# A fifth mixed pair in the second FFN's gate and up tiles, its weight sums made in the mixer

## The chip, the cores and the metric

The kernel runs on one core of one Trainium2 chip (trn2). The metric is the device time of one execution in microseconds (us). Five engines matter here: PE (TensorE, matrix products), DVE (VectorE), ACT (ScalarE), POOL (GpSimd) and SP (SyncE, which here only issues transfers). Each works through its own instructions in order and waits on semaphores that other engines and transfers set. Transfers run on 16 DMA engines that all queues share.

## The reference

One layer of a decoder over 272 positions (16 meta tokens, 256 sequence positions), model width 2048, in float32:

```python
h += 0.5 * swiglu(rms_norm(h, g1), w_gate1, w_up1, w_down1)      # first FFN, hidden width 5632
z  = rms_norm(h, gm) @ w_in                                      # q, k, v, index keys, conv and gate columns
h += (sigmoid(ga) * y_attn + sigmoid(gc) * y_conv) @ w_out       # sparse attention and short gated convolution
h += 0.5 * swiglu(rms_norm(h, g2), w_gate2, w_up2, w_down2)      # second FFN
swiglu(x, g, u, d) = (silu(x @ g) * (x @ u)) @ d
```

The result is `h` without the meta tokens.

## The kernel before

**Precision.** Every float32 weight is split into a high part (`whi`, made by ACT at L175) and the rest (`wlo`, made by DVE at L176), and every product is three matmuls (high times high, high times low, low times high), for instance L408 to L410 in `trio`. So each weight passes through SP (load into a `raw` buffer), ACT, DVE and PE. `Stream` (L109 on) keeps that order: weights come in *units* of at most 1024 columns. When PE's program takes a unit, `Stream.next` also emits the split of the unit three places further on (`AHEAD`). There are four pairs of `whi` and `wlo` buffers, three `raw` buffers of 1 MB, and a fourth (`raws`) in the second FFN. A load is issued once the split of the buffer's former weights is done.

**Extra work** is hung on the stream by unit number: `st.put` with a slot of `LAG` (the slot halved is the number of units to wait; even slots go before the split of that step in the engines' order, odd ones behind it), `st.later` likewise.

**The stages.** First FFN (to about 790 us), norm and keys (`pkv`), index queries (`pi`), queries (`pq`), convolution (`pxc`, `pcg`, `pb`), with the attention's small steps laid between, one a unit; then gates and branches, the output projection, and the second FFN from 1412 us.

**The second FFN** works on tiles of 512 columns, 6 and then 5 gate and up tiles (`GROUPS`), each group followed by its share of the down projection in two tiles. A gate and up tile takes the 2048 input features in eight *pairs* of 128-wide blocks. For a pair, gate and up for two blocks of 128 tokens are a 2 by 2 times 2 by 2 block product. A *plain* pair does it with eight products (24 matmuls of 512 columns, units named 0 and 1). A *mixed* pair does it in Winograd's way with seven (21 matmuls, units A to D, where A, C and D are 1024 columns and B is 512). For that it needs sums of the activations (`combos`: five sums on DVE, and splits of them on ACT and DVE, kept in `comb` and elsewhere), and sums of the weights: units A and B use three of the four weight blocks as they are (0.75 MB), C and D four sums (1 MB) that were made earlier and lie in DRAM scratch (`made`). When a tile's last mixed pair is through, `spread` and `gather` put the products together; then come silu, the product with up, two transposes and `move_blocks`, which writes the tile to DRAM (`hold<-mt`, POOL) and reads it back turned (four times `mt<-hold`, POOL).

**Which pairs are mixed** is the table `MIXED = 1, 3, 5, 6`; the very first tile mixes pair 5 alone. `order(n, mixed)` (L89) lists a tile's units in the pairs' order 0 to 7.

**The weight sums** are made by `job` (L554): a POOL transfer brings the 1 MB chunk into a buffer, four DVE operations of 128x512 (L568) make the sums, a POOL transfer writes them to scratch. `JOBS = 46` of the 57 jobs run in the first FFN, one every five units, with three buffers. The last 11 run behind the convolution.

Of the kernel before, what the change touches and what calls it, by code (L numbers as in the profile page):

```python
# [15 lines left out]
P = 128  # L16
# [9 lines left out]
H = 8  # L26
# [43 lines left out]
FIFTH = 4  # L70
FIVE = ()
LAST_MORE = 3, 4
JOBS_FROM = 24
JOBS_EVERY = 5
JOBS = 46
LATE_FROM = 4
LATE_EVERY = 6
# [5 lines left out]
    act_combos=(4, 12, 19, 32), factors=(7, 10, 12), out=(1, 1, 5, 17), act_split=(9, 14, 25, 33),  # L83
    below=(12, 17, 22, 30, 34), below_split=(15, 20, 30, 34, 35), fifth=(22, 25), late_below=(0, 5),
    late_split=(0, 6),
)


def order(n, mixed):  # L89

    out, i = [], 0
    while i < n:
# [4 lines left out]
        i += 1  # L97
    return out
# [137 lines left out]
def tile_decoder_layer(  # L236
# [53 lines left out]
    for g, n in enumerate(GROUPS):  # L290
        for f in range(n):
            now = sorted((*MIXED, *(FIFTH,) * ((g, f) in FIVE))) if gu else FIRST_MIXED
            sums = {i: scratch.tile([P, RAW], F32, name=f"made{gu + i}") for i in now}
            made += [(wgu2[gu + i], x) for i, x in sums.items()]
            for i, name in order(8, now):
                st.add_part(name, wgu2[gu + i], sums.get(i))
            gu += 8
        for d in (0, 2):
            now = down_mixed(g, d)
            sums = {i: scratch.tile([P, RAW], F32, name=f"sums{down + i}") for i in now}  # L300
            made += [(wd2[down + i], x) for i, x in sums.items()]
            for i, name in order(2 * n, now):
                st.add_part(name, wd2[down + i], sums.get(i))
            down += 2 * n
# [106 lines left out]

    def quads(c, m, x, mixed, n, after_mixed, tail=False):

        def of(k, j):
            return lambda part: x(k, j, part)

        plan, joined = [], []
        for i, name in order(n, mixed):
            k = 2 * i
            if name in "01":  # L420
                unit = [(c[j, q], of(k + int(name), j), 1 - q) for j in (1, 2) for q in (1, 0)]
                if tail and i == n - 1:
# [9 lines left out]
            plan.append((unit, i == max(mixed) and name == "D"))  # L432
# [120 lines left out]

    def job(pool, bufs, src, to, at, every, touch):  # L554
        box = {}

        def load():
            box["x"] = pool[0].tile([P, RAW], F32, name="made", bufs=bufs)
            if touch:
                nc.vector.tensor_copy(box["x"][:, :1], ones[:, :1])  # L560
            nc.gpsimd.dma_start(box["x"], src)

        def sums(n):
            b12, b11, b22, b21 = (box["x"][:, i * HALF : (i + 1) * HALF] for i in range(4))
            to, a, b, op = (
                (b22, b22, b12, "sub"), (b12, b12, b11, "sub"), (b11, b22, b11, "add"), (b21, b21, b11, "sub")
            )[n]
            getattr(nc.vector, f"tensor_{op}")(to, a, b)  # L568

        st.later(load, 1, at)  # L570
        for n in range(4):
            st.later(lambda n=n: sums(n), 1, at + every + n)
        st.later(lambda: nc.gpsimd.dma_start(to, box["x"]), 1, at + every + 4)

    def ffn_features():
# [3 lines left out]
        with tc.tile_pool(name="ffn1", bufs=2, reuse_waits="tile") as fp:  # L579
# [15 lines left out]

            for i, (src, to) in enumerate(made[:JOBS]):
                job([fp], 3, src, to, st.at + JOBS_FROM + i * JOBS_EVERY - 1, JOBS_EVERY, i < 3)

# [55 lines left out]
    def ffn_tokens():  # L654

        with ExitStack() as pools:
# [209 lines left out]
            for g, n in enumerate(GROUPS):  # L866
                for f in range(n):
# [15 lines left out]
                    quads(c, m, lambda k, j, part: known(("act", k // 4), act_tokens(k, j, part)), now, 8, lambda m=m: put(spread(m), LAG["spread"]))  # L883
                    put(gather(x, c), LAG["gather"])
# [29 lines left out]
                for d in (0, 2):  # L914
# [10 lines left out]

                    quads(c, m, middle_tokens, now, 2 * n, after, g and d)
                    put(gather_down(d, x, c, g == 1), LAG["drain"] if not g else 4 * (0,))
# [23 lines left out]
    with ExitStack() as mix:  # L951
# [250 lines left out]
        def scores(p, lag):  # L1202
            px = aux_tile("psc")
            for a in range(2):
                hh = 2 * p + a
                for j in (1, 2):
                    at = META * (2 - j)
                    nc.tensor.matmul(
                        px[:, a, SIDE[j]],
                        qT[:, hh, (j - 1) * P : j * P],  # L1210
                        kall[:, hh // (H // G), at : at + SEEN[j]],
# [69 lines left out]


        def q_steps():
            left = len(steps)
# [11 lines left out]
            new += [prep[3], tops[3], prep[4], tops[4], visit(prep[5], tops[5]), tops[6]]  # L1296
            new += [visit(*[lambda j=j: turn(qT, j) for j in (1, 2)]), tops[7], mask]
            for i in range(left):
# [46 lines left out]
        def conv_b(c, pb, y):  # L1345
            t = mw.tile([P, SEQ], F32, name="t", tag="cy")
            joined(t, pb)
            nc.vector.tensor_mul(y, t, y)
            to = cs[c // 4][:, c % 4]
            split_into(to[:, 0, :], to[:, 1, :], y)  # L1350

        for c in range(KC):
            box = {}
# [21 lines left out]
        st.later(jobs_pool, 3)  # L1375
        for i, (src, to) in enumerate(made[JOBS:]):
            job(jobs, 2, src, to, st.at + LATE_FROM + i * LATE_EVERY, LATE_EVERY, i < 2)

# [236 lines left out]
```

## Time and profile before

| | |
|---|---|
| time of 3 runs | 2108.28, 2108.98, 2109.17 us; median 2108.98 |
| profiled execution, first to last instruction | 2106.9 us |
| so outside the span, against the median of the runs | 2.1 us |
| granted PE clock | 1.00 |
| PE busy | 2098.8 us |
| DVE busy | 1582.4 us |
| ACT busy | 1058.9 us |
| bytes moved | 575.64 MB, 273 GB/s on average |

The profiled execution's own time is known only by its span. In the profile, a PE matmul of 512 columns is shown with a length of 0.39 us, but they overlap: one begins every 0.227 us. So the number of matmuls in a window is a better measure than their lengths. DVE and ACT operations of a row overlap a little too: two `wlo` in a row end 1.13 us apart where each is shown with 1.22 us. "L176" is a line of the kernel before; the changed kernel's lines lie a few further down.

### The profile page before, as it was taken

Reading aid. Unit: us, or ns where it says so; the run is one execution under the profiler, and the core shown is the slowest. Engines: PE = TensorE matmul, PEld = TensorE weight load, DVE = VectorE, ACT = ScalarE, POOL = GpSimd, SP = SyncE. Lnnn points to the kernel's source line nnn. Section 1 sums busy time; section 2 is a strip of 40 time slices with the busy share of each in tenths; the row PEclk is TensorE's granted clock in tenths of the full one; section 3 lists DMA queues with packets and bytes.
Section 4 is the critical chain, followed back from the end, with each engine's and each line's share of the span. In section 5 each row is a group of like instructions: output and inputs, shape, how many; then the busy total and the mean of one; then the engine's idle time right before and its main releaser. Section 6 shows DMA issues by size and latency. Waiting matters only on the chain.

```text
span 2106.9 us, 31863 instructions
## 1 busy us (share of the span) xinstructions
PE 2098.8 (100%) x12731; PEld 1889.9 (90%) x12731; DVE 1582.4 (75%) x2144; ACT 1058.9 (50%) x1342; POOL 106.0 (5%) x207
## 2 busy tenths in 40 slices
PE   9999999999999999999999999999999999999998
PEld 9999999999999999889988888888888888888887
DVE  7676766676776766578679678769788896878897
ACT  6444433344444445565444444456575565566654
POOL 0000000000000000000000000011000000000000
PEclk9999999999999999999999999999999999999999
DMA  7788888888888865445468886667988777799865
GB/s 265 260 320 327 324 315 322 311 337 310 322 313 325 328 224 177 164 159 181 152 216 329 323 301 223 219 233 255 314 314 300 281 268 247 282 306 319 306 250 207
DMA packets 85908, 575.64 MB, mean 273 GB/s; under 512 B 10112, under 2 KB 10880, under 8 KB 23808
## 3 DMA queue, kind: packets, MB, share of 16 engines
q1 hardware_dynamic: 64080, 438.34, 58.4%
q0 software_dynamic: 21104, 134.23, 17.1%
q8 instruction: 99, 1.62, 0.3%
q10 hardware_dynamic: 576, 1.05, 0.1%
q14 instruction: 49, 0.40, 0.1%
HBM read 504.90 MB, written 68.68 MB: 272 GB/s over the span
## 4 chain that ended last, share of the span: by engine, by line
PE 98%; DVE 1%; DMA 1%; issue 0%; ACT 0%; DVEq 0%; ACTq 0%
PE three L409 5%; PE three L408 5%; PE three L410 5%; PE pd L375 4%; PE pd L376 4%; PE pd L374 4%; PE pu L374 4%; PE pg L375 4%; PE pg L374 4%; PE pu L375 4%; PE pg L376 4%; PE pu L376 4%; PE pgt L402 3%; PE pgt L404 3%; PE pgt L403 3%; PE one L408 3%
## 5 line engine op out<-in xcount | busy, mean ns | idle before, releaser
L176 DVE TENSOR_TENSOR wlo<-raw,whi 128x1024 fp32r<-128x1024 f32 (+1 forms) x771 | 906.2, 1188 | 464.5 <-ACT whi L175 457.7
L175 ACT ACTIVATE whi<-raw 128x1024 fp32r<-128x1024 f32 (+1 forms) x771 | 786.4, 1030 | 883.4 <-PE pd L375 146.2
L375 PE MATMUL pd<-mid,whi 128*128 128x272 f32 x704 | 201.9, 287 | 0.0
L376 PE MATMUL pd<-mid,wlo 128*128 128x272 f32 x704 | 201.9, 287 | 0.0
L374 PE MATMUL pd<-mid,whi 128*128 128x272 f32 x704 | 201.9, 287 | 0.0
L374 PE MATMUL pu<-act,whi 128*128 128x272 f32 x672 | 192.8, 287 | 0.0
L376 PE MATMUL pu<-act,wlo 128*128 128x272 f32 x672 | 192.7, 287 | 0.0
L376 PE MATMUL pg<-act,wlo 128*128 128x272 f32 x672 | 192.7, 287 | 0.0
L375 PE MATMUL pg<-act,whi 128*128 128x272 f32 x672 | 192.7, 287 | 0.0
L375 PE MATMUL pu<-act,whi 128*128 128x272 f32 x672 | 192.7, 287 | 0.0
L374 PE MATMUL pg<-act,whi 128*128 128x272 f32 x672 | 192.7, 287 | 0.0
L568 DVE TENSOR_TENSOR made<-made 128x512 f32<-128x512 f32 x228 | 156.3, 685 | 0.0
L408 PE MATMUL three<-whi,act 128*128 128x512 f32 x352 | 137.2, 390 | 0.1
L409 PE MATMUL three<-wlo,act 128*128 128x512 f32 x352 | 137.0, 389 | 0.0
L410 PE MATMUL three<-whi,act 128*128 128x512 f32 x352 | 137.0, 389 | 0.0
L376 PEld LDWEIGHTS pd<-mid,wlo 128*128 128x128 f32 x704 | 132.7, 188 | 0.0
L374 PEld LDWEIGHTS pd<-mid,whi 128*128 128x128 f32 x704 | 132.7, 188 | 0.0
L375 PEld LDWEIGHTS pd<-mid,whi 128*128 128x128 f32 x704 | 132.7, 188 | 0.0
L176 DVE TENSOR_TENSOR wlo<-raws,whi 128x1024 fp32r<-128x1024 f32 x92 | 103.5, 1140 | 31.7 <-ACT whi L175 31.0
L374 PEld LDWEIGHTS pu<-act,whi 128*128 128x128 f32 x672 | 126.7, 188 | 0.0
L374 PEld LDWEIGHTS pg<-act,whi 128*128 128x128 f32 x672 | 126.7, 188 | 0.0
L376 PEld LDWEIGHTS pg<-act,wlo 128*128 128x128 f32 x672 | 126.6, 188 | 0.0
(381 smaller groups left out, 4482.7 us busy)
## 6 DMA issues: line engine op xcount, KB each, us to landing
raw<-in_wgu_dram SPq DMA_DIRECT2D x123, 1024.0 KB, 6.4
raw<-in_wd_dram SPq DMA_DIRECT2D x63, 1024.0 KB, 6.7
made<-in_wgu_dram POOLq DMA_DIRECT2D x41, 1024.0 KB, 10.6
made<-made POOLq DMA_DIRECT2D x41, 1024.0 KB, 6.5
raw<-made SPq DMA_DIRECT2D x31, 1024.0 KB, 6.1
raw<-in_wcv_dram SPq DMA_DIRECT2D x24, 1024.0 KB, 4.9
raw<-in_wgc_dram SPq DMA_DIRECT2D x24, 1024.0 KB, 5.1
raw<-in_wga_dram SPq DMA_DIRECT2D x24, 1024.0 KB, 5.4
```

The lines of the kernel that those rows point to most:

```text
L175: nc.scalar.activation(hi[:, :n], raw, AF.Copy)
L176: nc.vector.tensor_sub(lo[:, :n], raw, hi[:, :n].bitcast(F32))
L374: nc.tensor.matmul(ps, whi, xhi, start=first, stop=False)
L375: nc.tensor.matmul(ps, whi, xlo, start=False, stop=False)
L376: nc.tensor.matmul(ps, wlo, xhi, start=False, stop=last)
L402: nc.tensor.matmul(ps, xhi, whi, start=k + i == 0, stop=False)
L403: nc.tensor.matmul(ps, xhi, wlo, start=False, stop=False)
L404: nc.tensor.matmul(ps, xlo, whi, start=False, stop=k + i == n - 1)
L408: nc.tensor.matmul(ps, x(0), w[0], start=first, stop=False)
L409: nc.tensor.matmul(ps, x(0), w[1], start=False, stop=False)
L410: nc.tensor.matmul(ps, x(1), w[0], start=False, stop=last)
L568: getattr(nc.vector, f"tensor_{op}")(to, a, b)
```

## The change

It does three things.

1. Pair 4 becomes a fifth mixed pair (`FIFTH`) in ten of the eleven gate and up tiles, all but the very first. Its activation sums go into the buffer `below` at the start of the second tile of the first group, and once more at the start of the second group's first tile, since the down projection uses `below` in between.
2. The pairs are taken in the order 0, 1, 3, 2, 4, 5, 6, 7 (`CHUNKS`) in all eleven tiles: plain, mixed, mixed, plain, three mixed, plain.
3. The ten weight chunks more need ten jobs more. `MID_JOBS = 10` run from the keys to the convolution, every five units from the fourth unit on (units counted from the keys), the last two at 48 and 58. Their buffers are the places of tiles that aren't in use yet: the queries' transposed tile (`tB`) and the second half of the convolution's output (`c1`), in turn. So the tiles `qT` and `cs` are now made when they are first written.

```diff
-FIVE = ()
+CHUNKS = 0, 1, 3, 2, 4, 5, 6, 7
+FIVE = (*((0, f) for f in range(1, GROUPS[0])), *((1, f) for f in range(GROUPS[1])))
 JOBS = 46
+MID_JOBS = 10
+MID_FROM = 3
+MID_EVERY = 5
-    ... fifth=(22, 25), ...
+    ... fifth=(5, 5, 7, 7, 9, 11, 11, 13, 13), ...
...
-            now = sorted((*MIXED, *(FIFTH,) * ((g, f) in FIVE))) if gu else FIRST_MIXED
+            now = [i for i in CHUNKS if i in MIXED or (i == FIFTH and (g, f) in FIVE)] if gu else FIRST_MIXED
...
-            for i, name in order(8, now):
+            for i, name in order(CHUNKS, now):
...
-                        put(fns, 5 * (LAG["fifth"][0],) + 4 * (LAG["fifth"][1],))
-                    quads(c, m, ..., now, 8, lambda m=m: put(spread(m), LAG["spread"]))
+                        put(fns, LAG["fifth"])
+                    quads(c, m, ..., now, CHUNKS, lambda m=m: put(spread(m), LAG["spread"]))
...
-        qT = mp.tile([P, H, SEQ], F32, name="qT", tag="tB")
+        late_tiles = {}
-        cs = [mp.tile([P, KC // 2, 2, SEQ], F32R, name=f"cs{i}", tag=f"c{i}") for i in range(2)]
+        for i, (src, to) in enumerate(made[JOBS : JOBS + MID_JOBS]):
+            job(
+                lambda i=i: mp.tile([P, RAW], F32, name="made", tag=("tB", "c1")[i % 2 if i < 8 else 1]), src, to,
+                st.at + MID_FROM + (i + max(i - 7, 0)) * MID_EVERY, MID_EVERY, i < 2,
+            )
...
+        def place_q():
+            late_tiles["qT"] = mp.tile([P, H, SEQ], F32, name="qT", tag="tB")
...
-        for i, (src, to) in enumerate(made[JOBS:]):
+        for i, (src, to) in enumerate(made[JOBS + MID_JOBS :]):
```

How the instructions stand now, at the three places that the prediction speaks of:

**SP, the loads of one gate and up tile.** The third tile of the first group: 2048 columns are a whole chunk (a plain pair), 1536 the three blocks for A and B, `made` the sums for C and D. Before, from pair 0 to pair 6:

```order
L152 DMA raws<-in_wgu_dram 128x2048
L152 DMA raw<-in_wgu_dram 128x1536
L152 DMA raw<-made_79 128x2048
L152 DMA raw<-in_wgu_dram 128x2048
L152 DMA raws<-in_wgu_dram 128x1536
L152 DMA raw<-made_80 128x2048
L152 DMA raw<-in_wgu_dram 128x2048
L152 DMA raw<-in_wgu_dram 128x1536
L152 DMA raws<-made_81 128x2048
L152 DMA raw<-in_wgu_dram 128x1536
L152 DMA raw<-made_82 128x2048
```

Now:

```order
L155 DMA raw<-in_wgu_dram 128x2048
L155 DMA raw<-in_wgu_dram 128x1536
L155 DMA raw<-made_80 128x2048
L155 DMA raws<-in_wgu_dram 128x1536
L155 DMA raw<-made_81 128x2048
L155 DMA raw<-in_wgu_dram 128x2048
L155 DMA raw<-in_wgu_dram 128x1536
L155 DMA raws<-made_82 128x2048
L155 DMA raw<-in_wgu_dram 128x1536
L155 DMA raw<-made_83 128x2048
L155 DMA raw<-in_wgu_dram 128x1536
L155 DMA raws<-made_84 128x2048
```

Pair 3's two loads have moved ahead of pair 2's; then six loads for three mixed pairs stand in a row, where a whole chunk for a plain pair 4 stood first.

**DVE, the second tile of the first group, pairs 1 to 3.** `wlo` is the split of a unit. Before, behind the two transposes that end the former tile's work, only splits stand there, one behind the other:

```order
L794 TENSOR_TENSOR few<-u,few 128x1024
L637 STREAM_TRANSPOSE mt<-few 128x4x4x32 x2
L176 TENSOR_TENSOR wlo<-raw,whi 128x1024 x4
L176 TENSOR_TENSOR wlo<-raws,whi 128x1024
L176 TENSOR_TENSOR wlo<-raws,whi 128x512
L176 TENSOR_TENSOR wlo<-raw,whi 128x1024 x5
```

Now the fifth pair's sums (L709 to L713, in `few`) and splits (L696, into `below`) stand between the splits of pair 3:

```order
L179 TENSOR_TENSOR wlo<-raw,whi 128x1024 x2
L709 TENSOR_TENSOR few<-act 128x512
L710 TENSOR_TENSOR few<-few 128x128
L179 TENSOR_TENSOR wlo<-raw,whi 128x1024
L711 TENSOR_TENSOR few<-few 128x128
L712 TENSOR_TENSOR few<-few 128x128
L179 TENSOR_TENSOR wlo<-raw,whi 128x512
L713 TENSOR_TENSOR few<-few 128x128
L179 TENSOR_TENSOR wlo<-raws,whi 128x1024
L696 TENSOR_TENSOR below<-few,below 128x128
L179 TENSOR_TENSOR wlo<-raws,whi 128x1024
L696 TENSOR_TENSOR below<-few,below 128x3x128
```

The ten operations (the sums of five rows and two splits, L696 with an ACT operation ahead of each) come after the first two splits, those of pair 1's C and D.

**DVE, queries to convolution.** Where the queries' norm is taken (`rs_y`, `rs_z`, `hrr`; `keys` is the choice of the largest scores) and the convolution's first chunk begins (`cx`). Before:

```order
L176 TENSOR_TENSOR wlo<-raw,whi 128x1024
L503 RECIPROCAL rs_y<-rs_z 128x16
L504 TENSOR_TENSOR rs_z<-rs_y 128x16
L505 TENSOR_TENSOR rs_z<-rs_z,rs_v 128x16
L506 TENSOR_SCALAR rs_z<-rs_z 128x16
L507 TENSOR_TENSOR hrr<-rs_y,rs_z 128x16
L1186 MAX m_10224<-keys 128x8
L1187 MATCH_REPLACE keys<-m_10224,keys 128x144
L176 TENSOR_TENSOR wlo<-raw,whi 128x1024
L1329 TENSOR_TENSOR cx<-pcg,cx 128x258
L982 TENSOR_TENSOR zz_8894<-zz_8894,small 128x1024
```

Now:

```order
L179 TENSOR_TENSOR wlo<-raw,whi 128x1024
L572 TENSOR_TENSOR made<-made 128x512
L507 RECIPROCAL rs_y<-rs_z 128x16
L508 TENSOR_TENSOR rs_z<-rs_y 128x16
L509 TENSOR_TENSOR rs_z<-rs_z,rs_v 128x16
L510 TENSOR_SCALAR rs_z<-rs_z 128x16
L511 TENSOR_TENSOR hrr<-rs_y,rs_z 128x16
L1197 MAX m_10287<-keys 128x8
L1198 MATCH_REPLACE keys<-m_10287,keys 128x144
L179 TENSOR_TENSOR wlo<-raw,whi 128x1024
L572 TENSOR_TENSOR made<-made 128x512
L1345 TENSOR_TENSOR cx<-pcg,cx 128x258
```

The eighth job's four sums stand behind four splits in a row, one sum behind each; two of them are in these rows.

More of the change, by code (lines that the diff above doesn't have):

```diff
@@ L83, with order @@
     act_combos=(4, 12, 19, 32), factors=(7, 10, 12), out=(1, 1, 5, 17), act_split=(9, 14, 25, 33),
-    below=(12, 17, 22, 30, 34), below_split=(15, 20, 30, 34, 35), fifth=(22, 25), late_below=(0, 5),
+    below=(12, 17, 22, 30, 34), below_split=(15, 20, 30, 34, 35), fifth=(5, 5, 7, 7, 9, 11, 11, 13, 13), late_below=(0, 5),
     late_split=(0, 6),
 )
-def order(n, mixed):
-    out, i = [], 0
-    while i < n:
+def order(chunks, mixed):
+    out = []
+    for i in chunks:
         if i not in mixed:
@@ L301, in tile_decoder_layer @@
             made += [(wd2[down + i], x) for i, x in sums.items()]
-            for i, name in order(2 * n, now):
+            for i, name in order(range(2 * n), now):
                 st.add_part(name, wd2[down + i], sums.get(i))
@@ L410, in trio, with quads @@
         nc.tensor.matmul(ps, x(1), w[0], start=False, stop=last)
-    def quads(c, m, x, mixed, n, after_mixed, tail=False):
+    def quads(c, m, x, mixed, chunks, after_mixed, tail=False):
         def of(k, j):
@@ L417, in quads @@
         plan, joined = [], []
-        for i, name in order(n, mixed):
+        last_mixed = [i for i in chunks if i in mixed][-1]
+        for i, name in order(chunks, mixed):
             k = 2 * i
@@ L431, in quads @@
                 unit = [(*p, b) for b, p in enumerate(unit[name])]
-            plan.append((unit, i == max(mixed) and name == "D"))
+            plan.append((unit, i == last_mixed and name == "D"))
         flat = [id(p[0]) for unit, _ in plan for p in unit]
@@ L552, in start_tiles, with job @@
         return four
-    def job(pool, bufs, src, to, at, every, touch):
+    def job(place, src, to, at, every, touch):
         box = {}
         def load():
-            box["x"] = pool[0].tile([P, RAW], F32, name="made", bufs=bufs)
+            box["x"] = place()
             if touch:
@@ L596, in ffn_features @@
             for i, (src, to) in enumerate(made[:JOBS]):
-                job([fp], 3, src, to, st.at + JOBS_FROM + i * JOBS_EVERY - 1, JOBS_EVERY, i < 3)
+                job(
+                    lambda: fp.tile([P, RAW], F32, name="made", bufs=3), src, to,
+                    st.at + JOBS_FROM + i * JOBS_EVERY - 1, JOBS_EVERY, i < 3,
+                )
             two = [aux_tile(f"start{i}") for i in range(2)]
@@ L881, in ffn_tokens @@
                         fns = combos(halves, FIFTH, [below[:, 1, :1], below[:, 0]], "fifth")
-                        put(fns, 5 * (LAG["fifth"][0],) + 4 * (LAG["fifth"][1],))
-                    quads(c, m, lambda k, j, part: known(("act", k // 4), act_tokens(k, j, part)), now, 8, lambda m=m: put(spread(m), LAG["spread"]))
+                        put(fns, LAG["fifth"])
+                    quads(c, m, lambda k, j, part: known(("act", k // 4), act_tokens(k, j, part)), now, CHUNKS, lambda m=m: put(spread(m), LAG["spread"]))
                     put(gather(x, c), LAG["gather"])
@@ L924, in after @@
                         put([lambda q=q: halves_to(ht[d + q], ends if q else u[:, 1:3]) for q in range(2)], LAG["half"])
-                    quads(c, m, middle_tokens, now, 2 * n, after, g and d)
+                    quads(c, m, middle_tokens, now, range(2 * n), after, g and d)
                     put(gather_down(d, x, c, g == 1), LAG["drain"] if not g else 4 * (0,))
@@ L1296, in q_steps @@
             new += [prep[3], tops[3], prep[4], tops[4], visit(prep[5], tops[5]), tops[6]]
-            new += [visit(*[lambda j=j: turn(qT, j) for j in (1, 2)]), tops[7], mask]
+            new += [visit(
+                place_q, *[lambda j=j: turn(late_tiles["qT"], j) for j in (1, 2)]
+            ), tops[7], mask]
             for i in range(left):
@@ L1375, in tile_decoder_layer @@
         st.later(jobs_pool, 3)
-        for i, (src, to) in enumerate(made[JOBS:]):
-            job(jobs, 2, src, to, st.at + LATE_FROM + i * LATE_EVERY, LATE_EVERY, i < 2)
+        for i, (src, to) in enumerate(made[JOBS + MID_JOBS :]):
+            job(
+                lambda: jobs[0].tile([P, RAW], F32, name="made", bufs=2), src, to,
+                st.at + LATE_FROM + i * LATE_EVERY, LATE_EVERY, i < 2,
+            )
         m = [mp.tile([P, 2, 2, 512], F32, name=f"m{i}", tag=t) for i, t in enumerate(("tA", "tB"))]
```

10 lines of the change are left out of this document (7 added, 3 removed).

## The prediction, made before the changed kernel was timed

> **What bounds the kernel now.** I read the page's busy times and the chain of work that ended last, then tile by tile the windows of the second FFN, then the waits and transfers in them.
>
> ```profile
> span 2106.9 us, 31863 instructions
> PE 2098.8 (100%) x12731; PEld 1889.9 (90%) x12731; DVE 1582.4 (75%) x2144; ACT 1058.9 (50%) x1342; POOL 106.0 (5%) x207
> ...
> PE 98%; DVE 1%; DMA 1%; issue 0%; ACT 0%; DVEq 0%; ACTq 0%
> ```
>
> PE works from end to end, and the last chain is PE's own work to 98%. So a matmul less is time less, and a delay elsewhere costs only what is longer than the lead that the splits have over PE. Two gate and up tiles of the second FFN, as windows from one tile's first matmul to the next's, and a stretch where loads fill the DMA engines (columns: PE, weight loads, DVE, ACT, POOL busy, granted clock, busy share of the DMA engines, GB/s):
>
> ```profile
> 1502.60:1543.40 40.80, 40.80 (x181) 33.78 (x180) 33.66 (x36) 25.62 (x29) 2.74 (x5) 1.00 0.89 310
> 1584.30:1625.10 40.80, 40.80 (x181) 33.80 (x180) 34.07 (x36) 25.88 (x29) 2.73 (x5) 1.00 0.87 310
> 1580.00:1585.00 5.00, 5.00 (x24) 4.14 (x23) 4.96 (x7) 1.73 (x3) 0.00 (x0) 1.00 0.98 386
> ```
>
> Four mixed pairs of 21 matmuls and four plain ones of 24 make 180 in 40.8 us: 0.2267 us each, at clock 1.00, without a stall. DVE is busy for 33.7 to 34.1 us of it (83%), the DMA engines for 0.87 to 0.89. Both have little left, so the question is what they do to the gain.
>
> **The gain.** Ten pairs of 24 matmuls become pairs of 21; the order of the two programs shows 30 fewer on PE. 30 x 0.2267 = **-6.8 us**. A mixed pair lasts 4.76 us, a plain one 5.44.
>
> **DVE and ACT in a tile.** Per tile a pair of two 1024-wide splits becomes one of three and a 512-wide one.
>
> ```profile
> L176 DVE TENSOR_TENSOR wlo<-raw,whi 128x1024 fp32r<-128x1024 f32 x720 | 873.5, 1224 | 460.8 <-ACT whi L175 454.1
> L175 ACT ACTIVATE whi<-raw 128x1024 fp32r<-128x1024 f32 x720 | 756.8, 1059 | 858.5 <-PE pd L375 146.2 <-PE pu L375 139.2 <-PE pg L375 137.3
> L568 DVE TENSOR_TENSOR made<-made 128x512 f32<-128x512 f32 x228 | 156.3, 685 | 0.0
> ...
> 1590.27 4.59 DVE L176 TENSOR_TENSOR wlo<-raw,whi 128x1024 fp32r<-128x1024 f32 x4
> ```
>
> That is 1.5 x 1.22 = 1.8 us more DVE work in a tile that is now 40.1 us long: 35.5 to 35.9 us, 89%. The last row, of the timeline, shows four splits in a row in 4.59 us: with 1.22 for the last, they end 1.12 us apart. So in a row of mixed pairs the splits alone take 3 x 1.13 + 0.6 = 4.0 us of each pair's 4.76, and ACT's less. Where a tile begins, DVE puts the former tile together, and the splits come latest at pair 1; behind them now stands mixed pair 3 instead of plain pair 2, and it gains 0.2 us or more on each 1024-wide unit (1.36 us of PE against 1.13). I cost this at nothing; the cover is the splits' lead, and where it is used up the terms below say so.
>
> **The fifth pair's activation sums**, in two tiles. The first unit behind which they stand is pair 1's D; its split and the matmul that takes it, in the second tile of the first group and in the second group's first tile:
>
> ```profile
> 1468.94 1.21 DVE L176 TENSOR_TENSOR wlo<-raw,whi 128x1024 fp32r<-128x1024 f32 x1
> 1470.84 0.39 PE L409 MATMUL two<-wlo,comb 128*128 128x512 f32 x1
> ...
> 1799.06 1.22 DVE L176 TENSOR_TENSOR wlo<-raw,whi 128x1024 fp32r<-128x1024 f32 x1
> 1800.57 0.39 PE L409 MATMUL two<-wlo,comb 128*128 128x512 f32 x1
> ```
>
> The leads are 0.69 and 0.29 us. The same kind of sums, elsewhere, with the split behind them:
>
> ```profile
> 1704.22 0.68 DVE L702 TENSOR_TENSOR few<-mid 128x512 f32<-128x512 f32 x1
> 1704.94 0.29 DVE L703 TENSOR_TENSOR few<-few 128x128 f32<-128x128 f32 x1
> 1705.27 0.29 DVE L704 TENSOR_TENSOR few<-few 128x128 f32<-128x128 f32 x1
> ...
> 1705.88 1.22 DVE L176 TENSOR_TENSOR wlo<-raw,whi 128x1024 fp32r<-128x1024 f32 x1
> ```
>
> The first two take 1.05 us from start to start, the other three 0.61; I put the splits into `below` at 0.1 to 0.5 as far as they show. Unit by unit, lead plus PE's time for the unit ahead minus DVE's: pair 3's A: 0.69 + 1.36 - 1.05 - 1.13 = -0.13; B: 1.36 - 0.41 - 0.61 = +0.34; C: 0.34 + 0.68 - 0.21 - 1.13 = -0.32; D about -0.07; pair 2's first unit -0.25; then it recovers. Negative values are PE waiting: 0.8 us in one tile, 1.2 us in the other. **+2.0 us**; bounds: 0, and all 2.3 us of this work twice, 4.6.
>
> **The ten jobs from keys to convolution.** Forty operations of 0.685 us, and 20 MB. DMA has room there. Here are the stretch from the keys on, and the one from the convolution's start:
>
> ```profile
> 797.00:922.00 125.00, 125.00 (x701) 106.69 (x700) 80.17 (x173) 64.69 (x101) 0.53 (x2) 1.00 0.50 172
> 922.00:974.00 52.00, 52.00 (x391) 49.64 (x390) 44.42 (x94) 31.17 (x65) 2.21 (x3) 1.00 0.51 175
> ```
>
> In the first, seven jobs add about 19 us to 80 of 125: hidden. In the second DVE has 7.6 us left of 52, nearly all before 934 us. From the timeline two operations of DVE with the idle time ahead of them, then the latest split there and the matmul that takes it, and the split and matmul at the ninth job's place:
>
> ```profile
> 927.85 1.23 DVE L176 TENSOR_TENSOR wlo<-raw,whi 128x1024 fp32r<-128x1024 f32 x1 [2.43 <-ACT whi L175]
> ...
> 936.10 1.23 DVE L982 TENSOR_TENSOR zz<-zz,small 128x1024 f32<-128x1024 f32 x1 [0.42 <-ACT zz L981]
> ...
> 943.91 1.22 DVE L176 TENSOR_TENSOR wlo<-raw,whi 128x1024 fp32r<-128x1024 f32 x1
> ...
> 945.58 0.28 PE L386 MATMUL pb<-act,wlo 128*128 128x256 f32 x1
> ...
> 956.75 1.21 DVE L176 TENSOR_TENSOR wlo<-raw,whi 128x1024 fp32r<-128x1024 f32 x1
> ...
> 959.80 0.28 PE L376 MATMUL pcg<-act,wlo 128*128 128x258 f32 x1
> ```
>
> The lead is 0.45 us, and the eighth job's four sums now stand 10 to 20 us ahead of it. The first falls into DVE's 2.43 us of idle time before 927.85; the second delays `rs_v` and with it ACT; the third delays `hrr`, the fourth what follows: 3 x 0.6 to 0.685, less the idle 0.42 us before 936.10, is 1.4 to 1.6 us against 0.45. **+1.1 us**; bounds 0 and 4 x 0.685 - 0.45 = 2.3. The ninth job's sums come one by one over four units where the lead is 1.8 us (959.80 less 957.97), and I cost them at nothing; without that cover, up to 2.7.
>
> **The loads of a tile.** Five mixed pairs need 5 x 1.75 + 3 = 11.75 MB instead of 11. Alone, 1 MB takes 4.8 us to land. But in each of nine tiles `move_blocks` of the tile before runs beside them. Here is the tile at 1584: the issues of pair 4's chunk and pair 5's A (two issues), of pair 5's sums, and of the four reads; then the transfers' times to landing, beside those of the tile at 1502:
>
> ```profile
> 1592.61 2.60 SPq L152 DMA_DIRECT2D raw<-in_wgu_dram  x2
> 1596.62 0.33 SPq L152 DMA_DIRECT2D raws<-made  x1
> ...
> 1594.68 2.18 POOL L648 DMA_DIRECT2D mt<-hold  x4 [3.49 <-ACT whi L175]
> ```
>
> ```profile
> raw<-made SPq DMA_DIRECT2D x1, 1024.0 KB, 4.8
> ...
> raws<-made SPq DMA_DIRECT2D x1, 1024.0 KB, 10.0
> ...
> raws<-made SPq DMA_DIRECT2D x1, 1024.0 KB, 12.5
> ```
>
> So pair 5's sums, behind the move's start, take 10.0 and 12.5 us instead of 4.8. Now pair 4's sums and pair 5's stand there, and no plain pair lies in between. In the tile at 1502 ACT waited for such a load, and PE took the unit just in time; the last row is that of the waits of the whole second FFN:
>
> ```profile
> 1527.52 1.06 ACT L175 ACTIVATE whi<-raws 128x1024 fp32r<-128x1024 f32 x1 [2.84 <-DMA raws<-made]
> 1528.62 1.23 DVE L176 TENSOR_TENSOR wlo<-raws,whi 128x1024 fp32r<-128x1024 f32 x1 [2.60 <-ACT whi L175]
> ...
> 1530.04 0.39 PE L409 MATMUL three<-wlo,act 128*128 128x512 f32 x1
> ...
> ACT whi L175 <- DMA raws<-made: 8.6, 4, 3.3
> ```
>
> A landed load can be used 2.3 us later at the earliest (1.1 + 1.2). Count from a tile's first matmul. Loads land in the order of issue, so I take it that the same bytes land at the same times. Pair 5's sums ended 2.75 MB counted from pair 4's load on, and had landed 1596.62 + 10.0 - 1584.3 = 22.3 us into this tile and 1527.4 - 1502.6 = 24.8 into the other (1527.52 is when ACT could begin). Now these bytes are pair 4's two loads, pair 5's A and a quarter of its sums; the rest, 0.79 million bytes, takes 2.0 us more at the 386 GB/s of the third window above: 24.3 and 26.8. PE comes to pair 5's C at 2 x 5.44 + 3 x 4.76 + 2.04 = 27.2 and to its first `wlo` one matmul (0.2) later, so the sums have to land by 27.4 - 2.3 = 25.1. So the first kind of tile keeps 0.8 us, the second loses 1.7. Four of the eleven tiles show the late kind (8.6 us in 4 waits). I take 1 us in each of four, as some are less late: **+4.0 us**. Bounds: 0, and 1.9 us in all nine, 17.
>
> By the Trainium skill, "DMA: Bandwidth & Descriptors", section "Anatomy of one DMA — SWDGE (gpsimd) path", a transfer takes 2.0 us and its bytes at 436 GB/s, for 1 MB 4.4 us. By it nothing would be late, and the sum would be -3.7 us instead of +0.3. The row of a load alone (4.8) agrees with it, the rows beside the move (10.0, 12.5) do not, and the same page's section "Queues, rings and completion order" says that an engine takes queues in turn packet by packet, which fits them; I go by the rows.
>
> **The sum.** -6.8 + 2.0 + 1.1 + 4.0 = +0.3: span 2107.2 us, and with the 2.1 us that the median of the runs stands above the profiled span, **2109.3 us**. A difference under 0.2% (4.2 us) can't be told from none in this kernel, so the forecast is no change.
>
> **The rivals.**
>
> *All of it hidden.* For it: no stall of PE over 0.1 us in ten of eleven tiles, and seven of them with loads in time. Against: the leads of 0.3 to 0.7 us above. Then -6.8: 2102.2 us. All that keeps the three costs under 2.6 us belongs here (down from 2104.8).
>
> *The loads late in every tile.* Place: pair 4's sums to pair 6, behind the move's reads. Once the splits have lost their lead, DVE at 4.0 of 4.76 us a pair plus two writes into `mid` doesn't get it back before the tile ends. From 0.9 us per tile on (9 x 0.9 = 8) the kernel is slower by over 0.2%. At 1.9 us: -6.8 + 2.0 + 1.1 + 17.1 = +13.4, 2122 us. For it: the DMA share of 0.87 to 0.89 goes up with 0.75 MB more in less time. Against: seven tiles are not late today.
>
> *The jobs' transfers late.* A place is loaded one unit after its last store, so store and load must fit in seven units of 2.7 us (the stretch of 125 us has 46):
>
> ```profile
> made<-in_wgu_dram POOLq DMA_DIRECT2D x41, 1024.0 KB, 10.6
> made<-made POOLq DMA_DIRECT2D x41, 1024.0 KB, 6.5
> ```
>
> 17.1 of 19.0 us, at the first FFN's load. If two of the late jobs make DVE wait 3 us each in the tight stretch, +6: 2115 us. Against: DMA is half idle there.
>
> That the change doesn't do what it says is excluded by the 30 matmuls that are gone.
>
> **Chances.** No change within 0.2%: 0.45 (own range 2104.8 to 2113.2). Faster (all or most hidden): 0.34. Slower: 0.21, of it 0.17 loads, 0.04 jobs. The range begins at 2101.8, just under the whole gain, and ends at 2115.5, which leaves out the loads late in most tiles.
>
> **What would show it.** Right: ten tiles of 177 matmuls; PE waiting for `wlo` or `whi` near pairs 4 to 6 in some tiles, with ACT waiting for `raws<-made` or `raw<-made` ahead of it; waits of about 1 us at pair 3 in two tiles, and one at the convolution's first chunk. Wrong: tiles of 40.1 us throughout (all hidden), or tiles above 41 (late everywhere).

## The result, and the profile after

The changed kernel takes 2129.89 us (median of 4 runs, 2127.40 to 2131.47) against 2108.63 us of the kernel before beside it (2107.85 to 2109.17): a ratio of 1.0101, 95% interval 1.0087 to 1.0116. It is slower by 21 us where the forecast was no change.

The page of the changed kernel, with the chain of work that ended last:

```profile
span 2129.3 us, 31995 instructions
PE 2108.9 (99%) x12701; PEld 1881.4 (88%) x12701; DVE 1626.4 (76%) x2220; ACT 1073.9 (50%) x1366; POOL 117.6 (6%) x227
...
PE 79%; DVE 9%; DMA 7%; issue 2%; ACT 2%; DVEq 0%; ACTq 0%
```

The 30 matmuls are gone (12701 for 12731), and yet the span is 22.4 us longer. The chain, PE to 98% before, now runs through DVE and transfers for 16%. Where the 22.4 us lie, from the first matmul of each stage in the two traces (the second FFN's first matmul stands at 1418.9 us before and at 1424.0 after; the rows are rounded):

| stage | change, us |
|---|---|
| first FFN, to the keys | +0.3 |
| keys, index queries, queries | +0.4 |
| convolution with the attention in it | +3.3 |
| gates, branches, output projection | +1.2 |
| second FFN: 30 matmuls fewer | -6.8 |
| its tiles (0,1) and (1,0), beyond their matmuls | +1.6 |
| its other eight tiles with a fifth pair, beyond their matmuls | +23.9 |
| its last down projection | -0.8 |
| behind the last matmul | -0.4 |

(0,1) is the second tile of the first group, (1,0) the second group's first. In what follows a tile's *excess* is the time from its first matmul to the next tile's, less the number of its matmuls times 0.22667 us (40.80 us over 180). Before, it is 0.04 us in nine of these ten tiles and 0.43 in (1,0). After, tile by tile: 0.77, 2.01, 2.25, 3.99, 5.01 in the first group, and 1.25, 2.13, 2.53, 3.31, 3.00 in the second. Two of the tiles as windows (PE, weight loads, DVE, ACT, POOL busy, granted clock, DMA share, GB/s), and below them four waits of the second FFN with total, count and longest:

```profile
1507.80:1549.90 42.10, 41.52 (x179) 32.81 (x178) 34.75 (x37) 27.14 (x31) 2.74 (x5) 1.00 0.93 313
1592.30:1636.40 44.10, 41.89 (x179) 32.71 (x178) 36.47 (x39) 27.10 (x31) 2.75 (x5) 1.00 0.89 306
...
ACT whi L178 <- DMA raw<-made: 34.9, 11, 7.0
PEld three L412 <- DVE wlo L179: 20.8, 38, 1.1
...
ACT whi L178 <- DMA raw<-in_wgu_dram: 15.4, 14, 2.2
...
ACT whi L178 <- DMA raws<-made: 10.7, 4, 5.0
```

177 matmuls need 40.1 us and take 42.1 to 44.1. DVE's busy time is close to what was forecast (34.8 and 36.5 us), and the DMA engines move about the 310 GB/s of before although they are busier. For loads of sums alone ACT waits 45.6 us in 15 waits; before it was 8.6 in 4. The first late load of the stage, in the tile at 1507.77: its issue, its time to landing, the high split that waited for it, DVE behind that, and PE.

```profile
1517.83 0.33 SPq L155 DMA_DIRECT2D raws<-made  x1
...
raws<-made SPq DMA_DIRECT2D x1, 1024.0 KB, 10.6
...
1528.53 2.01 ACT L178 ACTIVATE whi<-raws 128x1024 fp32r<-128x1024 f32 x2 [4.97 <-DMA raws<-made]
...
1529.62 2.36 DVE L179 TENSOR_TENSOR wlo<-raws,whi 128x1024 fp32r<-128x1024 f32 x2 [4.90 <-ACT whi L178]
...
1530.90 0.50 PE L412 MATMUL three<-wlo,below 128*128 128x512 f32 x1 [0.30 <-DVE wlo L179]
...
1531.57 1.06 ACT L178 ACTIVATE whi<-raw 128x1024 fp32r<-128x1024 f32 x1 [1.03 <-DMA raw<-in_wgu_dram]
...
1542.15 1.06 ACT L178 ACTIVATE whi<-raw 128x1024 fp32r<-128x1024 f32 x1 [1.98 <-DMA raw<-in_wgu_dram]
```

These are pair 4's sums (PE multiplies them with `below`). They land 20.7 us into the tile and are first needed, by the prediction's own reckoning, at 2 x 5.44 + 2 x 4.76 + 2.04 + 0.2 - 2.3 = 20.3. So the first late load is late by only 0.4 us, and its tile ends with an excess of 2.0. What follows are late loads again: the last two rows are ACT's waits for pair 5's A and for pair 7's chunk.

The same holds for the other tiles. From pair 4 on, PE waits 21 times in the eight tiles for over 0.1 us, and each time the split that it waits for ends 2.4 to 2.5 us after its load landed, little more than the 2.3 us of the two splits alone. The units from pair 4 on hold 17.9 of the 24.2 us. The other 6.3 stand in a tile's first four pairs, and there ACT waits for no load. In the tile at 1549.89, PE waits at pair 1 for splits that stand on DVE behind the former tile's transposes, though their load had landed 8.1 us earlier:

```profile
1555.71 1.30 DVE L644 STREAM_TRANSPOSE mt<-few 128x512 f32<-128x512 f32 x2
1556.94 2.32 DVE L179 TENSOR_TENSOR wlo<-raws,whi 128x1024 fp32r<-128x1024 f32 x2
...
1558.18 0.50 PE L412 MATMUL three<-wlo,act 128*128 128x512 f32 x1 [0.24 <-DVE wlo L179]
```

Six of the eight tiles have this wait, all but the first of each group: the two with a tile ahead of them in which PE waited for no load.

### The profile page after: what moved, and what is told of

Its sections match the earlier page's. It is cut to its first block, busy times and chain, and to the rows that moved or that the text cites. A ratio compares the mean times of both kernels' runs of the same rounds, so it can differ in the third digit from the quotient of the medians.

```text
span 2129.3 us, 31995 instructions
## 1 busy us (share of the span) xinstructions
PE 2108.9 (99%) x12701; PEld 1881.4 (88%) x12701; DVE 1626.4 (76%) x2220; ACT 1073.9 (50%) x1366; POOL 117.6 (6%) x227
## 4 chain that ended last, share of the span: by engine, by line
PE 79%; DVE 9%; DMA 7%; issue 2%; ACT 2%; DVEq 0%; ACTq 0%
DVE wlo L179 5%; DMA raw<-in_wgu_dram 5%; PE pd L377 4%; PE pd L378 4%; PE pd L379 4%; PE pu L379 4%; PE pg L379 4%; PE pu L377 4%; PE pg L377 4%; PE pg L378 4%; PE pu L378 4%; PE three L412 3%; PE three L413 3%; PE pgt L406 3%; PE pgt L405 3%; PE pgt L407 3%
## 5 line engine op out<-in xcount | busy, mean ns | idle before, releaser
L179 DVE TENSOR_TENSOR wlo<-raw,whi 128x1024 fp32r<-128x1024 f32 (+1 forms) x785 | 919.3, 1184 | 449.8 <-ACT whi L178 444.8
L178 ACT ACTIVATE whi<-raw 128x1024 fp32r<-128x1024 f32 (+1 forms) x785 | 797.3, 1026 | 860.5 <-PE pd L378 146.2
L572 DVE TENSOR_TENSOR made<-made 128x512 f32<-128x512 f32 x268 | 184.2, 687 | 2.5 <-DMA made<-in_wgu_dram 2.5
L411 PE MATMUL three<-whi,act 128*128 128x512 f32 x342 | 133.8, 391 | 1.6 <-DVE u L777 1.5
L413 PE MATMUL three<-whi,act 128*128 128x512 f32 x342 | 133.3, 390 | 0.0
L379 PEld LDWEIGHTS pu<-act,wlo 128*128 128x128 f32 x672 | 126.6, 188 | 0.0
L378 PEld LDWEIGHTS pg<-act,whi 128*128 128x128 f32 x672 | 126.6, 188 | 0.0
L377 PEld LDWEIGHTS pg<-act,whi 128*128 128x128 f32 x672 | 126.6, 188 | 0.0
```

The source lines that it names most:

```text
L178: nc.scalar.activation(hi[:, :n], raw, AF.Copy)
L179: nc.vector.tensor_sub(lo[:, :n], raw, hi[:, :n].bitcast(F32))
L377: nc.tensor.matmul(ps, whi, xhi, start=first, stop=False)
L378: nc.tensor.matmul(ps, whi, xlo, start=False, stop=False)
L379: nc.tensor.matmul(ps, wlo, xhi, start=False, stop=last)
L411: nc.tensor.matmul(ps, x(0), w[0], start=first, stop=False)
```

## The experiments

Theory L: the loads that are under way beside a moved tile's transfers come late. Theory D: three mixed pairs in a row leave DVE too little room for the splits. Theory O: the new order of the pairs does it. The first four runs tell these apart.

**The order and the jobs without the fifth pair.**

```diff
+            now = [i for i in CHUNKS if i in MIXED] if gu else FIRST_MIXED
+            both = [i for i in CHUNKS if i in now or (i == FIFTH and (g, f) in FIVE)]
+            sums = {i: scratch.tile([P, RAW], F32, name=f"made{gu + i}") for i in both}
...
-                    if (g, f) in FIVE:
-                        now[FIFTH] = fifth
...
```

> The changed kernel with pair 4 left plain in all tiles: the new order of the pairs and the ten jobs more stay, the fifth pair's sums are made and written but not used, and its activation sums are left out. Theory L (the fifth pair's loads come late beside the moved tile's transfers) and theory D (the splits of three mixed pairs in a row use up DVE): the second FFN takes its old 682.6 us to within 3 us, and the 5.1 us before it stay, so about 2114 us. Theory O (the order of the pairs alone makes the waits): the second FFN stays 10 us or more above its old time, 2124 or more.

2112.97 us, and no gate and up tile of the second FFN has an excess over 0.08 us. The second FFN is as long as before; the 4.9 us ahead of it stay. O falls.

**Without the move's transfers.**

```diff
     def move_blocks(x):
-        hold = scratch.tile([P, 4, 2, P], F32, name="hold", bufs=2)
-        nc.gpsimd.dma_start(hold, x)
...
+        pass
```

> The changed kernel without the five transfers of each moved tile (the write to DRAM and the four reads back are left out, so the second FFN's middle values stay unturned in all tiles but the last of each group); DVE, ACT and PE do the same work. Theory L: the excess of the nine tiles with a move, 25 us in all, falls to under 5, and the time to about 2108 to 2112 us. Theory D: the excess stays, within 4 us of the changed kernel's 2130.

2115.57 us. The excess of the eight tiles falls from 24.2 to 7.2 us (with (0,1) to 8.0, not under 5). So the move's transfers are the larger part of the loss, but not all. Behind a tile's fourth pair 3.0 us are left of 17.9: single loads still come late, as the two waits below show. In the first four pairs 4.2 are left of 6.3.

```profile
1508.24:1549.35 41.11, 40.68 (x179) 33.10 (x177) 35.62 (x38) 27.26 (x31) 0.00 (x0) 1.00 0.84 294
...
ACT whi L178 <- DMA raw<-in_wgu_dram: 6.7, 7, 1.9
ACT whi L178 <- DMA raw<-made: 4.8, 3, 2.5
```

**Half of pair 4's sums.**

```diff
-            self.loads.append((x, x.shape[1], ()))
+            self.loads.append((x, RAW // 2 if short and x is made else x.shape[1], ()))
...
-        a, b = {"0": (0, 2), ..., "C": (0, 2), "D": (2, 4)}[name]
+        a, b = {"0": (0, 2), ..., "C": (0, 2), "D": (0, 2) if short else (2, 4)}[name]
```

> The changed kernel where the load of pair 4's sums brings 0.5 MB instead of 1 (its unit D uses unit C's columns again, so the products of that pair are wrong); every instruction on PE, DVE and ACT stays. Theory L: 0.5 MB less in each tile's row of mixed pairs is 1.4 us at 386 GB/s and more beside the move, so the time falls by 10 to 20 us, to 2110 to 2120. Theory D: within 4 us of 2130.

2117.06 us: 13 us less for 0.5 MB less a tile, with the work of PE, DVE and ACT unchanged. The eight tiles' excess falls to 8.5, of which 2.2 stand behind the fourth pair and 6.3 in the first four. Both runs are against D as the main cause. They leave open whether the waits in the first four pairs, which are for DVE, come from late loads too.

**Three mixed pairs first.**

```diff
-CHUNKS = 0, 1, 3, 2, 4, 5, 6, 7
+CHUNKS = 0, 1, 3, 4, 2, 5, 6, 7
```

> The changed kernel with the pairs in the order 0, 1, 3, 4, 2, 5, 6, 7: the three mixed pairs in a row stand at the tile's start, whose loads are issued ahead of the moved tile's transfers, and only two mixed pairs follow beside it. Theory L: the excess of the tiles falls by a third or more, to 2113 to 2122 us. Theory D: DVE has the former tile's sums to make at a tile's start, so the waits grow: 2130 or more.

2148.18 us, so my expectation from L was wrong, and the time is on D's side. The trace says why, and it isn't DVE. In the tile at 1509.06 the plain pair behind the three mixed ones waits:

```profile
raws<-in_wgu_dram SPq DMA_DIRECT2D x1, 1024.0 KB, 11.0
...
1530.17 1.06 ACT L178 ACTIVATE whi<-raws 128x1024 fp32r<-128x1024 f32 x1 [4.88 <-DMA raws<-in_wgu_dram]
...
1531.28 0.50 PE L411 MATMUL one<-whi,act 128*128 128x512 f32 x1 [2.34 <-ACT whi L178]
1532.54 0.79 PE L412 MATMUL one<-wlo,act 128*128 128x512 f32 x1 [0.76 <-DVE wlo L179]
```

All nine tiles with a move wait at this place, each until 2.4 us after the load's landing, and 36 of the eight tiles' 38 us of excess stand here or later in the tile. This load beside the move takes 11 us, though it is a plain pair's. What decides is how long the buffers ahead of it last on PE. A chunk of a plain pair lasts 5.44 us, a buffer of a mixed pair 2.04 or 2.72, on average 2.38, so with mixed pairs four buffers come round in 9.5 us. Here only mixed pairs stood ahead. I had asked which loads stand beside the move; the question is what stands ahead of them. So L became: a load takes 9 to 12 us beside the move, and four buffers of mixed pairs don't last that long. The next run adds a buffer.

**A fifth raw buffer, in the second group.** Its five tiles leave the place of the first group's sixth tile of `mid` free.

```diff
+                if g:
+                    st.more_raw.append(fp.tile([P, RAW], F32, name="raws", tag="midx"))
                 for f in range(n):
...
-        raw = self.more_raw[0] if self.more_raw and not self.n_raw else self.raw_pool.tile(...)
+        own = self.n_raw < len(self.more_raw)
+        raw = self.more_raw[self.n_raw] if own else self.raw_pool.tile(...)
```

> The changed kernel with one more raw buffer of 1 MB from the second group on (the first group's sixth tile of middle values, unused then, gives the place), so five loads instead of four can be under way or wait to be split. Theory L, as the first four runs left it (a load beside the moved tile's reads takes 11 us, and four buffers of mixed pairs last PE only some 9.5 us): the four tiles of the second group with a move, 2.35 + 2.71 + 4.03 + 1.87 = 11.0 us longer than their matmuls, fall to under 4.5 together, the first group's five stay at 14 in all (10 to 17): 2121 to 2125 us. Theory D (DVE has too little room in three mixed pairs): the second group's four tiles stay above 9, about 2129.

2117.26 us. The second group's four tiles with a move have an excess of 0.04, 0.04, 0.15 and 0.04 us, together 0.3 instead of 11.0; the first group's four, still with four buffers in the same program, 10.5. The time is 4 us under what was expected. Two of those tiles, their waits for loads over the four tiles, and the load of pair 4's sums in the first of them:

```profile
1845.65:1885.81 40.16, 40.16 (x179) 33.22 (x177) 35.91 (x38) 27.39 (x31) 2.74 (x5) 1.00 0.93 340
1885.81:1925.97 40.16, 40.16 (x179) 33.22 (x177) 35.92 (x38) 27.38 (x31) 2.75 (x5) 1.00 0.91 330
...
ACT whi L179 <- DMA raws<-made: 0.8, 1, 0.8
ACT whi L179 <- DMA raw<-in_wgu_dram: 0.4, 1, 0.4
ACT whi L179 <- DMA raw<-made: 0.3, 1, 0.3
...
1858.40 0.33 SPq L156 DMA_DIRECT2D raw<-made  x1
...
raw<-made SPq DMA_DIRECT2D x1, 1024.0 KB, 9.9
```

The load still takes 9.9 us, but it is issued earlier, and nobody waits. DVE has the same 35.9 us of work in 40.16 and doesn't hold PE up, in the first four pairs either: D falls as a cause by itself. Where loads are on time, DVE is too.

**One buffer less, in the kernel before.**

```diff
-MORE_RAW = 1
+MORE_RAW = 0
```

> The kernel before with one raw buffer less in the second FFN (three instead of four). Theory L: a load beside the moved tile's reads takes 9 to 12 us, three buffers do not cover it even with four mixed pairs, so the nine tiles with a move lose at least 2 us each: 2127 us or more. If four mixed pairs left room to spare, nothing: 2109.

2162.87 us in one run, 54 us more than before, with an excess of 2.5 to 7.5 us in the nine tiles with a move, and waits for loads as in the changed kernel:

```profile
ACT whi L175 <- DMA raw<-in_wgu_dram: 53.3, 25, 3.9
...
ACT whi L175 <- DMA raw<-made: 34.9, 15, 4.0
```

So the kernel before has no buffer to spare. From both sides the number of buffers is shown to decide.

**Long rows in the move.**

```diff
-            nc.gpsimd.dma_start(x[q * 32 : q * 32 + 32], of_quarter[q])
+            nc.gpsimd.dma_start(x[q * 32 : q * 32 + 32], hold[q * 32 : q * 32 + 32])
```

> The changed kernel where the four reads of a moved tile bring the same bytes in rows of 4 KB (each partition its own, so the middle values are not turned) instead of 1 KB. Theory L with small pieces (the reads hold the DMA engines longer than their bytes do; the share is 1.0 and over where only 223 to 291 GB/s move): the excess of the nine tiles falls from 25 us to 8 to 15, 2113 to 2121 us. Theory L with bytes alone: the excess stays at 20 or more, 2126 to 2131.

2123.76 us, between the two. The four reads took 11.3 to 14.0 us from the first issue to the last landing in the eight tiles, with rows of 1 KB 12.0 to 14.1. The eight tiles' excess was 15.2 us, but the changed kernel's own second profile (below) has 15.9. That small pieces are what makes the reads slow isn't shown.

**Seven jobs, and no activation sums in the second group.**

```diff
-MID_JOBS = 10
+MID_JOBS = 7
...
-                    if (g, f) == (g, 1 - g) and any(at[0] == g for at in FIVE):
+                    if (g, f) == (0, 1):
```

> The changed kernel with seven of the ten jobs between keys and convolution and the other three among the late jobs; and the second group's activation sums of the fifth pair left out (its products take what the buffer holds, so they are wrong). If the eighth to tenth job make the loss ahead of the second FFN, that loss falls from 5.1 to 1.5 us or less; if the first seven do, it stays above 3.5. If the fifth pair's sums make the second group's first tile long, its excess falls from 1.25 to 0.5 us or less; if the loads do, it stays. The rest as in the changed kernel: 2124 to 2127 us.

2118.39 us. The loss ahead of the second FFN is 3.0 us, between the two cases, because this run is 1.6 us longer in the first FFN. From the keys to the gates it loses 0.3 us instead of 3.7, so the eighth to tenth job make that loss. The excess of (1,0) is 0.59 instead of 1.25, so the sums cost about 0.7 us there, by these two profiles. The tiles, whose instructions are the same as the changed kernel's, had an excess of 13.7 us instead of 24.2, which I hadn't expected. The next two runs ask about that.

**Seven jobs, nothing left out; and the changed kernel once more.**

```diff
-MID_JOBS = 10
+MID_JOBS = 7
```

> The changed kernel with seven of the ten jobs between keys and convolution and three among the late jobs, and everything else kept, the second group's sums too. From the run with seven jobs: 2119 us (its 2118.4 and 0.7 for the sums). From the changed kernel with only the three late jobs' loss taken away (3.2 us): 2127. Between them lies how much the waits in the tiles change from one program to the next with the same instructions there.

2122.53 us (ratio 1.0074, 1.0059 to 1.0089), with the loss between keys and gates at 0.2 us and the eight tiles' excess at 15.5.

> The changed kernel once more, for a second profile: if the waits in a tile are the same from run to run, the first group's four moving tiles lose 13 us again and the second group's 11; if they are not, the sums differ by several us while the time stays at 2127 to 2132.

2125.2 us in one run, 2.2 under the lowest of the four, with an excess of 9.9 us in the first group's four tiles and 6.0 in the second's, against 13.3 and 11.0 in the first profile. A tile of it:

```profile
1637.09:1679.44 42.35, 41.30 (x179) 32.84 (x178) 36.22 (x39) 27.12 (x31) 2.74 (x5) 1.00 0.91 321
```

So the waits in a tile change by up to 2.8 us from one execution of the same program to the next, and their sum by 8. The four profiles with these tiles (the changed kernel's two and those with seven jobs) lie at 13.7 to 24.2 us. A difference within that says nothing: neither the long rows nor the seven jobs can be told from the changed kernel by these tiles. A fall from 11.0 to 0.3 in one group, with the other as a control, is clear of it. The runs without the move and with half the sums, at 7.2 and 8.5, lie below all four, by one profile each.

**The fifth pair where there is a buffer for it.** The second group's five tiles only, with the fifth raw buffer, and five jobs.

```diff
-FIVE = (*((0, f) for f in range(1, GROUPS[0])), *((1, f) for f in range(GROUPS[1])))
+FIVE = (*((1, f) for f in range(GROUPS[1])),)
...
-MID_JOBS = 10
+MID_JOBS = 5
```

> A version made from what the runs showed: the fifth pair mixed in the second group's five tiles only, with the fifth raw buffer there, and five jobs between keys and convolution. Theory L: -3.4 us of matmuls, +0.6 for the jobs, +1 for the activation sums, +1 to 2 for what is still late: 2107 to 2109 us, the same as before. Theory D: the five tiles keep 9 us of waits, 2113 or more.

2106.84 us, ratio 0.9992 (0.9983 to 1.0002). Four tiles are at 0.04 us of excess, (1,0) at 2.65.

**The same with calmer places.** No job between keys and convolution (`MID_JOBS = 0`, so 16 late ones, and the tiles `qT` and `cs` made where they were), and the activation sums four units later:

```diff
-    ... fifth=(5, 5, 7, 7, 9, 11, 11, 13, 13), ...
+    ... fifth=(13, 15, 15, 17, 17, 19, 19, 21, 21), ...
```

> The fifth pair in the second group's five tiles with the fifth raw buffer, as before, but its five jobs are the last five of sixteen late jobs (none between keys and convolution, and the tiles of the queries and of the convolution's output are made where they were), and the activation sums of the fifth pair stand four units later in the second group's first tile. If the 1.4 us ahead of the second FFN and the 2.65 us in that tile came from these two places: -3.4 us of matmuls, -1.6 for the last down projection, +0.5 to +1.5 for the sums, so 2104 to 2105.5 us. If they came from elsewhere: 2106.5 or more.

2105.01 us (median of 11 runs, 2103.86 to 2106.11) against 2108.34 of 15 beside it: ratio 0.9984, interval 0.9975 to 0.9993: faster than the kernel before by 3.3 us. Now (1,0) has an excess of 0.08 us, the first of these two windows:

```profile
1792.95:1833.15 40.20, 40.20 (x178) 33.15 (x177) 37.56 (x45) 26.03 (x29) 0.00 (x0) 1.00 0.90 344
1833.15:1873.31 40.16, 40.16 (x178) 33.22 (x177) 35.92 (x38) 27.38 (x31) 2.75 (x5) 1.00 0.90 326
```

The last down projection is 1.6 us shorter too (0.67 us of excess instead of 2.30). It has 0.67 in all three programs with the fifth buffer and 1.4 or more in the others, so this part seems to be the buffer's. The kernel before with a fifth buffer and no fifth pair was not run, so how much of the 3.3 us the fifth pair itself brings isn't shown.

## Why the prediction was wrong

**The gain, -6.8 us: right.** With its loads in time, a tile of five mixed pairs takes 40.16 us.

**DVE and ACT in a tile, nothing: right as a price, but the cover mattered.** DVE's 35.9 us in 40.16 hold nobody up while loads are on time. But the splits take 4.0 of a mixed pair's 4.76 us, as the prediction says, so of a delay at most some 0.8 us a pair can come back. In the changed kernel DVE was behind at the start of six of the eight tiles, and the first four pairs lost 6.3 us in all. The prediction says of its rival, and not of its forecast, that a lost lead doesn't come back before the tile ends.

**The activation sums, +2.0 us: right in mechanism and nearly in size.** Measured 0.73 us in (0,1), where 0.8 was forecast, and 0.7 to 0.8 in (1,0), where 1.2 was. PE waits at pair 3's A and C and at pair 2's first unit, as the forecast has it; the largest of these waits is the first in (1,0):

```profile
1817.58 0.50 PE L412 MATMUL three<-wlo,act 128*128 128x512 f32 x1 [0.31 <-DVE wlo L179]
```

**The jobs, +1.1 us: too small, 3.3 measured.** The step that failed is "the ninth job's sums ... I cost them at nothing", and that the tenth was not looked at. The eighth job did what was forecast: PE waits for `wlo` at the convolution's first chunk, the first row here. The others hold up something else:

```profile
947.09 0.38 PE L389 MATMUL pb<-act,wlo 128*128 128x256 f32 x1 [0.59 <-DVE wlo L179]
...
964.80 0.68 DVE L572 TENSOR_TENSOR made<-made 128x512 f32<-128x512 f32 x1
965.40 0.28 DVE L1010 TENSOR_TENSOR zz<-rot 128x128 f32<-128x128 f32 x1
...
965.94 0.44 PE L1142 MATMUL pqt<-ident,zz 128*128 128x128 f32 x2 [0.88 <-DVE zz L1011]
...
997.51 1.23 DVE L572 TENSOR_TENSOR made<-made 128x512 f32<-128x512 f32 x1
...
999.64 0.42 ACT L468 ACTIVATE cs<-cy 128x256 fp32r<-128x256 f32 x1 [3.98 <-DVE cy L1364]
...
1001.00 1.12 PE L1287 MATMUL ppv<-pTx,vts 128*128 128x512 f32 x2 [0.95 <-ACT pTm L1274]
```

The ninth job's last sum stands right ahead of the queries' rotation (`zz<-rot`), which PE's transposes wait for. The tenth's stands ahead of the convolution's `cy`, which ACT waits for, and the attention's `pTm` is behind that on ACT. The three waits delay PE by 1.0, 1.0 and 1.3 us. I had compared only the splits with the matmuls that take them; an operation on DVE can be late for other readers on PE too. The 1.2 us from the gates to the output projection were not forecast. They are there in every program of this study with more weight sums, the last version included. No wait of over 0.1 us is behind them in either trace; single matmuls begin 0.24 us after the one before instead of 0.227. Why stays open.

**The loads, +4.0 us with bounds of 0 and 17: the step that decided.** Measured 24 us in one profile and 16 in the other. Three things in it failed.

First, only pair 5's sums were timed, since they were the late ones before. Pair 4's are due 4.8 us earlier, and the prediction doesn't ask whether they are there by then.

Second, "Loads land in the order of issue, so I take it that the same bytes land at the same times". By it pair 4's 1.75 MB would land with the first 1.75 MB of before, whose last load in the tile at 1502.6, the same tile before the change, is this one:

```profile
1513.20 0.33 SPq L152 DMA_DIRECT2D raw<-in_wgu_dram  x1
...
raw<-in_wgu_dram SPq DMA_DIRECT2D x1, 768.0 KB, 9.8
```

That is 1513.20 + 9.8 - 1502.6 = 20.4 us into the tile, due at 20.3, and they landed at 20.7: here the rule nearly held. Over the eight tiles it gives 17.3 to 20.7, at most 0.4 late, and measured are 20.7 to 23.6, late in every one. Part of that is the tile's own late start, but in the tile at 1848.01, which starts on time, it is 21.0 against 19.4. Loads do land in order, but beside the move's reads several are under way at once: in the tile at 1507.77 four that were issued 1.7 to 2.7 us apart took 10.6 to 10.9 us each.

Third, a tile's loss was taken as a single lateness, of at most 1.9 us. But a load that is late frees its buffer late, and a later load is issued late in turn: in the tile at 1507.77 pair 7's chunk is issued 27.4 us into the tile, where it was 26.2 in the tile ahead, which had no late load. So 0.4 us became 2.0 of excess there, and the later tiles of that profile reached 5.0.

The rival "the loads late in every tile" was the right case, at 2122 us and a chance of 0.17. It too went by one lateness per tile, and its loads are too small as well, 17.1 us against 24. What I counted against it, "seven tiles are not late today", said little: with one buffer less all of these tiles are late, so they stood near the edge already.

By the Trainium skill, "DMA: Bandwidth & Descriptors", section "Queues, rings and completion order", a DMA engine takes turns between the queues it has work for, packet by packet. The rows fit that for the move's reads beside the loads; no run here tries it by itself. By the same page of the Trainium skill, section "Anatomy of one DMA — SWDGE (gpsimd) path", a transfer that GpSimd issues takes 2.0 us and its bytes at 436 GB/s, by estimate 4.4 us for 1 MB. The loads here are issued by SP; one alone took 4.8 us, and the 10.6 us beside the move are 2.4 times that estimate.

## What to carry to other kernels

Price a stream of loads by its look-ahead: the time that the buffers ahead of a load last on the engine that eats them, against the load's time beside the worst neighbour, not its time alone. An edit by which the engine finishes a buffer sooner shortens that look-ahead, and a lateness of tenths in one load became a loss of 2 us in its tile here, since each later load is issued only when a buffer comes free. Whether a stream is at that edge can be asked by taking a buffer away: this kernel lost 54 us by it, and had no room for the fifth pair's loads.

## What the runs showed that I hadn't expected

**The clock falls after two short waits.** In the first group's last tile PE waited 1.48 and 0.76 us with one matmul between. The matmuls behind are shown with 0.63 us instead of 0.39 and begin 0.43 us apart instead of 0.2267, for some 3 us:

```profile
1661.18 0.50 PE L411 MATMUL three<-whi,below 128*128 128x512 f32 x1 [1.48 <-ACT whi L178]
1662.44 0.79 PE L412 MATMUL three<-wlo,below 128*128 128x512 f32 x1 [0.76 <-DVE wlo L179]
1663.03 0.63 PE L413 MATMUL three<-whi,below 128*128 128x512 f32 x1
...
1660.00:1666.00 6.00, 4.06 (x10) 3.04 (x11) 4.66 (x5) 5.07 (x6) 0.00 (x0) 0.72 0.83 328
```

The granted clock was 0.72 in those 6 us. A single wait of 0.8 us has no such follow-up in the same trace. The lower clock costs some 1.4 of this tile's 5.0 us. In the run with three mixed pairs first it happened six times, once behind two waits of 0.76 us, and is part of that run's 2148 us. Two waits of 1.33 and 0.76 us in the run with one buffer less (at 1976 us) had no such follow-up, so the sum of the waits alone doesn't decide. The Trainium skill, "TensorE: Matmul & The Clock Gate", Part 1, has the half clock follow an idle window of about 3.4 us; here the clock fell with 2.2 us of waiting in two pieces.

**The DMA engines were busy and moved little.** While the move's reads run, they moved 267 GB/s at a busy share of 0.97, where loads alone moved 386 at 0.98 in the trace of before:

```profile
1606.90:1614.90 8.00, 8.00 (x37) 6.64 (x36) 3.74 (x4) 2.26 (x3) 0.00 (x0) 1.00 0.97 267
```

Rows four times as long did not make the reads shorter (11.3 to 14.0 us against 12.0 to 14.1), so what holds the engines there is open.

**One sum on DVE and one product on POOL took longer side by side.** The weight sum at 997.51 in the rows above took 1.23 us instead of 0.685, while POOL's multiplication for the convolution ran beside it and took 1.59 us instead of 0.75:

```profile
978.14 0.75 POOL L1359 TENSOR_TENSOR cy<-cy,few 128x256 f32<-128x256 f32 x1
996.60 1.59 POOL L1359 TENSOR_TENSOR cy<-cy,few 128x256 f32<-128x256 f32 x1 [17.71 <-DVE cy L1356]
```

All eight profiles with the tenth job in this place show the same two lengths. It wasn't tried by itself, so that each slows the other isn't shown.
